# Query projection of a hybrid encoder block: the rotary channels of all heads in one channel tile

## The chip, the cores and the metric

The kernel runs on one core of a Trainium2 chip. The metric is the device time of one launch in microseconds, on the slowest core, which here is the only one. TensorE (PE) does the matmuls, VectorE (DVE), ScalarE (ACT) and GpSimd (POOL) the work on vectors, and SyncE (SP) issues nearly all DMA transfers, in one queue.

## The reference, cut to what matters

One encoder block over S = 2048 tokens of width 1024, all in float32: a combined projection feeds windowed attention (8 query heads of 64 channels, 2 key/value heads) and a bidirectional chunked scan (SSD, 16 chunks of 128 tokens); both are normed, projected out and added, and a convolved gated feed-forward part (FFN) follows. What bears on the change is the partial rotary embedding: only the first 16 of a head's 64 channels are turned.

```
def apply_partial_rope(t, cos, sin):
    half = ROT_DIM // 2                      # ROT_DIM = 16, head width 64
    t1, t2, rest = t[..., :half], t[..., half:ROT_DIM], t[..., ROT_DIM:]
    return jnp.concatenate([t1 * c - t2 * s, t2 * c + t1 * s, rest], axis=-1)
...
    h = rmsnorm(x, norm1_g[l])
    proj = h @ w_in[l]
    q, k, v, z, xbc, dt_raw = jnp.split(proj, IN_SPLITS, axis=-1)
    attn = rmsnorm(windowed_attention(q, k, v, ...), attn_out_g[l])
```

## The kernel before

**Matmuls.** Every float32 operand is split into a high part (rounded to the matmul's type) and the low rest, and each product is three matmuls: high x high, high x low, low x high (`mm3`, L105 to L108). A split is an ACT cast and a subtraction on DVE or POOL; for weights these are L141 and L142.

**Tiles and halves.** The tokens are worked in two halves of 1024. The projection runs by channel tiles of 128 columns: eight for the scan's inputs (`C0` to `C7`, `conv_unit`), tile 8 for the keys, and tiles 9 to 12 for the queries, two heads of 64 channels in each. One tile and 512 tokens are a bank, 128x512 in PSUM (`pj`, or `pq` where two tiles are made together). `tok_pair` makes values, gates and time steps for 256 tokens (`tp` banks, L500 to L502).

**Rotary work.** `rope_bank` (L417 to L466) takes a bank of tiles 8 to 12. It loads a table of cosines and sines for all 128 rows (`cs`, 512 KB, L425; rows that are not turned have cosine 1 and sine 0). In half 0 the table is multiplied by the tokens' norm factor r (L428), which half 1 has in its input already. The sine half of a work tile `rw` is set to zero on POOL (L430), the bank is copied to its other half (ACT, L431), and four DMAs of 8 rows each bring the partner channels to their place (L433, L434). DVE multiplies the bank by the cosines, which frees PSUM (L436). `flush()` then runs what earlier banks had deferred, and the bank defers its own tail: POOL multiplies by the sines and adds (L446, L447), then the sum is split. A head has 64 rows, and its high and low parts shall lie above each other in 128 rows, so each bank takes two casts and two subtractions over 64x512 (L441, L443) and one write of 512 KB to `qs_d` (L454). Attention loads its chunk of 128 tokens from there (`aq`, L700). The key bank writes to `ks_d` (L463, L464) from more pieces.

**Buffers.** `rw` comes from a ring of five work buffers (`t1024`) that many stages share. `cs` comes from that ring, or, by the bank, from the two buffers `qs` and `ks` in which attention also holds its `aq` and `ak`.

**Order.** Two strings (`PLAN`) say in which order the units of each half are written down: `R8` to `R12` are rotary tiles, `W` and `t` the token work, `b`, `s` steps of the scans, `a` steps of attention, `H` and `Q` the out-projection; `P3` makes tiles 11 and 12 for the last 512 tokens, and the same pair for the 512 before them comes in the first feed-forward units. A scheduler then fixes one order per engine from its own model of durations, so a change in one place can move instructions of other stages. Half 0 has ten rotary banks (two each for tiles 11, 10, 12, 9, 8), half 1 ten more.

**Other names.** L571 to L641 are steps of the time-step chain and the scans' states, L735 to L780 attention, L875 and L880 the decay matrices `ab` of the scan (eight DVE steps of 128x128, then one exponential on ACT), L885 to L936 the scan's outputs, L997 the out-projection's sum, L1022 and L208 the second norm's product and split.

## Time and profile before

| | us |
|---|---|
| three runs | 2496.54, 2498.95, 2504.64 (median 2498.95) |
| the profiled execution | 2505.61 |
| its span | 2503.8 |
| PE busy | 2373.5 (95%) |
| DVE, POOL, ACT busy | 1761.6, 1126.9, 1088.3 |

The span is the time between the first and the last instruction of the one execution that was recorded; the 1.8 us more are launch and end. All times below are from that execution, in us from the start of its span. The projection of half 0 takes until about 240 us, half 1 with attention, scans and out-projection until about 690; what follows is the feed-forward part, with the rest of attention and scans beside it.

### The profile page before, as it was taken

The numbers are of one execution on the slowest core, as the hardware profiler recorded it, in microseconds if no ns is written. First come the engines' busy times: TensorE is split into PE (matmuls) and PEld (weight loads), VectorE is DVE, ScalarE is ACT, GpSimd is POOL, SyncE is SP. The second block draws the span as 40 slices with busy tenths as digits, with TensorE's granted clock in tenths as the row PEclk, the third lists the DMA queues.
The fourth block names the chain that finished last, engine by engine and source line by source line (L and its number), as shares of the span: only waits on it lengthen the run. The fifth ranks groups of instructions, "written<-read, shape, count | busy, mean of one in ns | idle before, by whom it ended". The sixth has DMA issues, their size and how long they took to land.

```text
span 2503.8 us, 31565 instructions
## 1 busy us (share of the span) xinstructions
PE 2373.5 (95%) x11440; PEld 1975.7 (79%) x11440; DVE 1761.6 (70%) x3116; ACT 1088.3 (43%) x1814; POOL 1126.9 (45%) x625
## 2 busy tenths in 40 slices
PE   8998999887899999999999999999999999999997
PEld 6877798766688887777788777777888877788887
DVE  5778778878786775468978685689686555844445
ACT  5444565444354444335444443254444433433334
POOL 1045314564545435445444443554444445544444
PEclk9999999998899999999999999999999999999998
DMA  6567445774433343333434333343443232332232
GB/s 225 178 198 224 126 147 186 247 246 149 141 116 122 127 140 97 101 112 122 126 131 137 99 133 114 90 129 119 129 127 96 84 114 89 118 101 93 93 94 84
DMA packets 176047, 332.13 MB, mean 133 GB/s; under 512 B 13202, under 2 KB 84242, under 8 KB 175892
## 3 DMA queue, kind: packets, MB, share of 16 engines
q1 hardware_dynamic: 175892, 330.12, 41.2%
q8 instruction: 90, 1.47, 0.2%
q14 instruction: 65, 0.53, 0.1%
HBM read 284.06 MB, written 44.71 MB: 131 GB/s over the span
## 4 chain that ended last, share of the span: by engine, by line
PE 50%; DVE 9%; POOL 2%; issue 2%; ACT 1%; DMA 1%; DVEq 0%; POOLq 0%; SPq 0%; ACTq 0%
PE up_b L108 9%; PE up_b L107 9%; PE up_b L106 9%; PE dn_b L106 3%; PE dn_b L107 3%; PE dn_b L108 3%; DVE fa L1047 2%; POOL wlo L142 2%; PE dn L107 2%; PE dn L106 2%; PE dn L108 2%; PE wo_b L108 2%; PE wo_b L106 2%; PE wo_b L107 2%; DVE m_lo L972 1%
## 5 line engine op out<-in xcount | busy, mean ns | idle before, releaser
L142 POOL TENSOR_TENSOR wlo<-wraw,whi 128x1024 fp32r<-128x1024 f32 (+1 forms) x306 | 739.0, 2416 | 901.8 <-ACT whi L141 849.8
L108 PE MATMUL up_b<-h_hi,wlo 128*128 128x512 f32 x1392 | 555.3, 399 | 15.9 <-POOL wlo L142 15.8
L107 PE MATMUL up_b<-h_lo,whi 128*128 128x512 f32 x1392 | 553.0, 398 | 4.7 <-DVE h_lo L208 4.7
L106 PE MATMUL up_b<-h_hi,whi 128*128 128x512 f32 x1392 | 554.3, 399 | 1.4 <-ACT whi L141 0.9
L141 ACT CAST whi<-wraw 128x1024 fp32r<-128x1024 f32 (+1 forms) x330 | 338.9, 1027 | 453.0 <-PE up_b L107 117.8
L1047 DVE SCALAR_TENSOR_TENSOR fa<-up_b,fcw,fa 128x511 f32<-128x511 f32 (+2 forms) x396 | 271.4, 686 | 206.1 <-ACT fa L1049 201.7
L108 PEld LDWEIGHTS up_b<-h_hi,wlo 128*128 128x128 f32 x1392 | 264.6, 190 | 79.8 <-POOL wlo L142 21.8
L107 PEld LDWEIGHTS up_b<-h_lo,whi 128*128 128x128 f32 x1392 | 264.3, 190 | 63.3 <-DVE h_lo L208 5.9
L106 PEld LDWEIGHTS up_b<-h_hi,whi 128*128 128x128 f32 x1392 | 264.1, 190 | 60.1 <-ACT whi L141 2.3
L106 PE MATMUL dn_b<-f,whi 128*128 128x512 f32 x528 | 211.4, 400 | 0.4 <-DVE x L1090 0.2
L107 PE MATMUL dn_b<-f,whi 128*128 128x512 f32 x528 | 208.8, 395 | 0.0
L108 PE MATMUL dn_b<-f,wlo 128*128 128x512 f32 x528 | 204.3, 397 | 0.0
L1069 ACT ACTIVATE fth<-fa 128x512 f32<-128x512 f32 (+1 forms) x88 | 55.6, 632 | 217.3 <-DVE fa L1047 165.3
L1074 ACT CAST f<-fth 128x512 fp32r<-128x512 f32 (+1 forms) x88 | 54.4, 620 | 207.6 <-DVE fth L1071 169.2
L1090 DVE TENSOR_TENSOR x<-x,dn_b 128x512 f32<-128x512 f32 x144 | 97.5, 680 | 61.0 <-PE dn_b L108 60.9
L1049 ACT ACTIVATE fa<-up_b,fcw 128x512 f32<-128x512 f32 x176 | 136.0, 774 | 0.2
L106 PEld LDWEIGHTS dn_b<-f,whi 128*128 128x128 f32 x528 | 99.7, 189 | 22.8 <-DVE x L1090 1.1
L108 PEld LDWEIGHTS dn_b<-f,wlo 128*128 128x128 f32 x528 | 99.3, 188 | 22.4 <-POOL wlo L142 0.3
L107 PEld LDWEIGHTS dn_b<-f,whi 128*128 128x128 f32 x528 | 99.2, 188 | 21.2
L875 DVE SCALAR_TENSOR_TENSOR ab<-ab,ldt,mask 128x128 f32<-128x128 f32 x256 | 106.7, 482 | 11.7 <-DMA ab<-acs_d 11.5
L1075 DVE TENSOR_TENSOR f<-fth,f 128x512 fp32r<-128x512 f32 (+1 forms) x88 | 79.2, 900 | 30.3 <-ACT f L1074 29.4
L106 PE MATMUL pj_b<-h_hi,whi 128*128 128x512 f32 x208 | 85.4, 411 | 12.3 <-ACT h_hi L235 7.1
(328 smaller groups left out, 5047.1 us busy)
## 6 DMA issues: line engine op xcount, KB each, us to landing
wraw<-in_w_up SPq DMA_DIRECT2D x176, 512.0 KB
wraw<-in_w_dn SPq DMA_DIRECT2D x64, 512.0 KB
wraw<-in_w_out SPq DMA_DIRECT2D x36, 512.0 KB
ab<-acs_d SPq DMA_DIRECT2D x32, 512.0 KB
wraw<-in_w_ch SPq DMA_DIRECT2D x28, 512.0 KB
wraw<-in_w_dn SPq DMA_DIRECT2D x32, 384.0 KB
ak<-ks_d SPq DMA_DIRECT2D x14, 768.0 KB
cs<-in_rope SPq DMA_DIRECT2D x20, 512.0 KB
```

The lines of the kernel that those rows point to most:

```text
L106: nc.tensor.matmul(ps, whi, xhi, start=first, stop=False)
L107: nc.tensor.matmul(ps, whi, xlo, start=False, stop=False)
L108: nc.tensor.matmul(ps, wlo, xhi, start=False, stop=last)
L141: A.copy(hi[:, :m], raw[:, :m])
L142: (V if i < WV or i in WVS else G).tensor_tensor(lo[:, :m], raw[:, :m], hi[:, :m].bitcast(F32), ALU.subtract)
L875: (G if i < SUBP[0 if first else 1] else V).scalar_tensor_tensor(ab[:, i, d], ab[:, i, d], ldt[:, d, c, h : h + 1], mask3[:, 2 * d * P : ( ...
L1047: V.scalar_tensor_tensor(o, src, w(q), o, ALU.mult, ALU.add)
L1049: A.activation(ai[:, 0:TB], u, AF.Identity, bias=w(3), scale=w(2))
L1069: A.activation(th[:, :n], acc[:, 0, :n], AF.Tanh)
L1074: A.copy(fs[:, idx, 0, :n], th[:, :n])
L1075: V.tensor_tensor(fs[:, idx, 1, :n], th[:, :n], fs[:, idx, 0, :n].bitcast(F32), ALU.subtract)
L1090: V.tensor_tensor(xv, xv, ps[i], ALU.add)
```

## The change

The host lays out the query columns differently. Tile 9 now holds the 16 rotary channels of all eight heads: rows 0 to 63 the first eight of each head, rows 64 to 127 the second eight. Tiles 10, 11 and 12 hold channels 16 to 31, 32 to 47 and 48 to 63 of all heads, and nothing in them is turned.

A bank of tiles 10 to 12 goes to the new `plain_bank`. In half 0 DVE multiplies it by r into a work tile `hl`; ACT casts, DVE subtracts, each once over 128x512, at once and not deferred; in half 1 both read the PSUM bank itself. Two writes of 256 KB (8 heads x 16 rows x 512 tokens) put high and low part in their rows of `qs_d`, whose layout is as before but for the order of the rows within a head's high and low part. There is no table, no zeroing, no swap and no POOL step. A bank of tile 9 has a table of its own (`ropeq`), two swaps of 64 rows instead of four of 8, no zeroing, one cast and one subtraction over 128x512, and four writes of 128 KB. Key banks (tile 8) are as before. Twelve of the sixteen query banks are plain. Over the kernel 12 table loads and 56 swaps go and 24 writes come.

```diff
--- before.py
+++ after.py
@@ -414,7 +414,23 @@
 
         pend.append(tail)
 
+    def plain_bank(ci, t0, u):
+        ts = slice(t0, t0 + 512)
+        half = t0 // 1024
+        hl = t1024(f"hl{ci}_{t0}").rearrange("p (a n) -> p a n", a=2)
+        if half in rbc:
+            V.tensor_tensor(hl[:, 1], u, rbc[half][:, t0 % 1024 : t0 % 1024 + 512], ALU.mult)
+            u = hl[:, 1]
+        flush()
+        A.copy(hl[:, 0].bitcast(F32R), u)
+        V.tensor_tensor(hl[:, 1].bitcast(F32R), u, hl[:, 0], ALU.subtract)
+        for s in range(2):
+            r0 = 64 * s + 16 * (ci - 9)
+            nc.sync.dma_start(qs_d[:, r0 : r0 + 16, ts], hl[:, s])
+
     def rope_bank(ci, t0, u, cs_tag=None):
+        if ci > 9:
+            return plain_bank(ci, t0, u)
         ts = slice(t0, t0 + 512)
         half = t0 // 1024
         if cs_tag is None:
@@ -422,16 +438,17 @@
         else:
             cs = bp.tile([P, 1536 if cs_tag == "ks" else 1024], F32, tag=cs_tag, name=f"cs{ci}_{t0}")[:, :1024]
         cs = cs.rearrange("p (a n) -> p a n", a=2)
-        nc.sync.dma_start(cs, a["rope"][:, :, ts])
+        nc.sync.dma_start(cs, a["rope" if ci == 8 else "ropeq"][:, :, ts])
         if half in rbc:
             r = rbc[half][:, t0 % 1024 : t0 % 1024 + 512]
             V.tensor_tensor(cs, cs, r.unsqueeze(1).broadcast_to([P, 2, 512]), ALU.mult)
         rw = t1024(f"rw{ci}_{t0}").rearrange("p (a n) -> p a n", a=2)
-        G.memset(rw[:, 1], 0.0)
+        if ci == 8:
+            G.memset(rw[:, 1], 0.0)
         A.copy(rw[:, 0], u)
-        for b in (0, 64):
-            nc.sync.dma_start(rw[b : b + 8, 1], rw[b + 8 : b + 16, 0])
-            nc.sync.dma_start(rw[b + 8 : b + 16, 1], rw[b : b + 8, 0])
+        for b, n in ((0, 8), (64, 8)) if ci == 8 else ((0, 64),):
+            nc.sync.dma_start(rw[b : b + n, 1], rw[b + n : b + 2 * n, 0])
+            nc.sync.dma_start(rw[b + n : b + 2 * n, 1], rw[b : b + n, 0])
         q = cs[:, 0]
         V.tensor_tensor(q, u, q, ALU.mult)
         flush()
@@ -447,11 +464,12 @@
             eng(16).tensor_tensor(q, q, rw[:, 1], ALU.add)
             lo, up = slice(0, 64), slice(64, 128)
             if ci != 8:
-                for e, (r0, r1) in enumerate(((lo, up), (up, lo))):
-                    put(rw[r0, e], q[r0])
-                    put(rw[r1, e], q[r0], rw[r0, e])
-                i = 2 * (ci - 9)
-                nc.sync.dma_start(qs_d[i : i + 2, :, ts].rearrange("a p t -> p a t"), rw)
+                put(rw[:, 0], q)
+                put(rw[:, 1], q, rw[:, 0])
+                for s in range(2):
+                    for z, rows in enumerate((lo, up)):
+                        r0 = 64 * s + 8 * z
+                        nc.sync.dma_start(qs_d[:, r0 : r0 + 8, ts], rw[rows, s])
                 return
             kl = bp.tile([P, 6 * P], F32, tag="vt", name=f"kl{t0}")[:, :512]
             for kv, (r0, r1) in enumerate(((lo, up), (up, lo))):
@@ -1434,7 +1452,10 @@
     r = {}
     r["x"] = f["x"][0]
     r["xT"] = np.ascontiguousarray(f["x"][0].T)
-    r["w_ch"] = tile_w(np.concatenate([w_in[:, 1280:2304], w_in[:, 512:640], w_in[:, 0:512]], 1))
+    wq = w_in[:, 0:512].reshape(D, H, HD)
+    qcols = [wq[:, :, 0:16].reshape(D, H, 2, 8).transpose(0, 2, 1, 3).reshape(D, P)]
+    qcols += [wq[:, :, i : i + 16].reshape(D, P) for i in (16, 32, 48)]
+    r["w_ch"] = tile_w(np.concatenate([w_in[:, 1280:2304], w_in[:, 512:640]] + qcols, 1))
     wt = np.concatenate([w_in[:, 640:1280], w_in[:, 2304:2320]], 1)
     r["w_t"] = np.ascontiguousarray(
         wt.reshape(NK, P, 2, TW).transpose(2, 1, 0, 3)
@@ -1472,6 +1493,9 @@
     rc[:, 0:8], rc[:, 8:16] = cos, cos
     rs[:, 0:8], rs[:, 8:16] = -sin, sin
     r["rope"] = np.stack([rc.reshape(P, S), rs.reshape(P, S)], 1)
+    qc = np.tile(cos, (2 * H, 1))
+    qsn = np.concatenate([np.tile(-sin, (H, 1)), np.tile(sin, (H, 1))], 0)
+    r["ropeq"] = np.ascontiguousarray(np.stack([qc, qsn], 1), dtype=np.float32)
     return r
 
 
```

What the scheduler makes of it is shown at three places, before and after apart (of L numbers above 430 the new file's are 16 to 18 higher).

DVE near the end of half 0's projection, before: `cs9` and `cs8` are the tables of R9 and K (the number behind is the bank's first token), `cacc` a convolution of tile 6.

```order
L436 TENSOR_TENSOR cs9_512_1635<-pj9_0_b1_1580,cs9_512_1635 128x512
L142 TENSOR_TENSOR wlo_1672<-wraw_1585,whi_1671 128x1024
L428 TENSOR_TENSOR cs9_0_1647<-cs9_0_1647,rx_half_150 128x1024
L366 SCALAR_TENSOR_TENSOR cacc6_0_1522<-cu6_0_1519,cacc6_0_1522 128x1024
L627 MEMSET stateb_3449 128x512
L436 TENSOR_TENSOR cs9_0_1647<-pj9_0_b0_1579,cs9_0_1647 128x512
L443 TENSOR_TENSOR rw9_512_1638<-cs9_512_1635,rw9_512_1638 64x512 x2
L443 TENSOR_TENSOR rw9_0_1650<-cs9_0_1647,rw9_0_1650 64x512 x2
L142 TENSOR_TENSOR wlo_2122<-wraw_1675,whi_2121 128x1024
L428 TENSOR_TENSOR cs8_512_1725<-cs8_512_1725,rx_half_150 128x1024
L436 TENSOR_TENSOR cs8_512_1725<-pj8_0_b1_1670,cs8_512_1725 128x512
```

The same place after:

```order
L453 TENSOR_TENSOR cs9_512_1563<-pj9_0_b1_1508,cs9_512_1563 128x512
L366 SCALAR_TENSOR_TENSOR cacc6_0_1457<-cu6_0_1454,cacc6_0_1457 128x1024
L444 TENSOR_TENSOR cs9_0_1572<-cs9_0_1572,rx_half_150 128x1024
L645 MEMSET stateb_3373 128x512
L142 TENSOR_TENSOR wlo_1595<-wraw_1513,whi_1594 128x1024
L453 TENSOR_TENSOR cs9_0_1572<-pj9_0_b0_1507,cs9_0_1572 128x512
L460 TENSOR_TENSOR rw9_512_1566<-cs9_512_1563,rw9_512_1566 128x512
L444 TENSOR_TENSOR cs8_0_1667<-cs8_0_1667,rx_half_150 128x1024
L460 TENSOR_TENSOR rw9_0_1575<-cs9_0_1572,rw9_0_1575 128x512
L444 TENSOR_TENSOR cs8_512_1648<-cs8_512_1648,rx_half_150 128x1024
L453 TENSOR_TENSOR cs8_512_1648<-pj8_0_b1_1593,cs8_512_1648 128x512
```

The scaling of `cs9_512` is no longer in the neighbourhood (it is 17th on the engine), R9's four subtractions are two, and K's first table is scaled ahead of R9's last subtraction.

SP's queue at the same place, before: the swaps of K's bank, R9's writes and K's tables.

```order
L434 DMA rw8_512_1728<-rw8_512_1728 8x512
L454 DMA qs_d_103<-rw9_512_1638 128x2x512
L425 DMA cs8_512_1725<-in_rope 128x2x512
L433 DMA rw8_512_1728<-rw8_512_1728 8x512
L434 DMA rw8_512_1728<-rw8_512_1728 8x512
L454 DMA qs_d_103<-rw9_0_1650 128x2x512
L425 DMA cs8_0_1743<-in_rope 128x2x512
```

After:

```order
L441 DMA cs8_0_1667<-in_rope 128x2x512
L450 DMA rw9_0_1575<-rw9_0_1575 64x512
L451 DMA rw9_0_1575<-rw9_0_1575 64x512
L472 DMA qs_d_103<-rw9_512_1566 8x8x512 x4
L441 DMA cs8_512_1648<-in_rope 128x2x512
L450 DMA rw8_512_1651<-rw8_512_1651 8x512
L451 DMA rw8_512_1651<-rw8_512_1651 8x512
L450 DMA rw8_512_1651<-rw8_512_1651 8x512
L451 DMA rw8_512_1651<-rw8_512_1651 8x512
L472 DMA qs_d_103<-rw9_0_1575 8x8x512 x4
```

One of K's tables is now ahead of R9's second swaps; the other stands behind four writes.

DVE in half 1, where tile 10's and tile 9's banks lie beside attention chunk 3 and the first scan chunks (`ab0`, `ab1`: their decay matrices), before:

```order
L443 TENSOR_TENSOR rw10_1024_4115<-cs10_1024_4113,rw10_1024_4115 64x512
L875 SCALAR_TENSOR_TENSOR ab1_0_4256<-ab1_0_4256,ldt_85,mask3_141 128x128 x6
L443 TENSOR_TENSOR rw10_1024_4115<-cs10_1024_4113,rw10_1024_4115 64x512
L875 SCALAR_TENSOR_TENSOR ab1_0_4256<-ab1_0_4256,ldt_85,mask3_141 128x128 x2
L436 TENSOR_TENSOR cs9_1536_4198<-pj9_1_b1_4143,cs9_1536_4198 128x512
L780 TENSOR_TENSOR am3_3693<-po3_1_3966,ao3_1_4016 64x256 x2
L875 SCALAR_TENSOR_TENSOR ab1_1_4258<-ab1_1_4258,ldt_85,mask3_141 128x128 x8
L516 SCALAR_TENSOR_TENSOR zth0_1_0_4314<-zth0_1_0_4314,tp0_1_0_b0_4264 128x200
L790 TENSOR_REDUCE ass3_4234<-asq3_4232 128x128
L622 TENSOR_TENSOR statef0_4036<-statef0_4036,stf0_4130 128x512
L436 TENSOR_TENSOR cs9_1024_4215<-pj9_1_b0_4142,cs9_1024_4215 128x512
```

After:

```order
L893 SCALAR_TENSOR_TENSOR ab0_0_3930<-ab0_0_3930,ldt_85,mask3_141 128x128 x8
L645 MEMSET statef_3911 128x512
L893 SCALAR_TENSOR_TENSOR ab0_1_3932<-ab0_1_3932,ldt_85,mask3_141 128x128 x8
L708 TENSOR_TENSOR sb5_3884<-sb5_3884,pbt5_3885 128x512
L453 TENSOR_TENSOR cs9_1536_4105<-pj9_1_b1_4050,cs9_1536_4105 128x512
L798 TENSOR_TENSOR am3_3617<-po3_0_3697,ao3_0_3880 64x256 x2
L785 TENSOR_TENSOR pl3_1_1_3907<-pt3_1_1_3900,ph3_1_1_3905 128x512
L785 TENSOR_TENSOR pl3_1_2_3920<-pt3_1_2_3913,ph3_1_2_3918 128x512
L453 TENSOR_TENSOR cs9_1024_4112<-pj9_1_b0_4049,cs9_1024_4112 128x512
L798 TENSOR_TENSOR am3_3617<-po3_1_3890,ao3_1_3940 64x256 x2
L893 SCALAR_TENSOR_TENSOR ab1_0_4151<-ab1_0_4151,ldt_85,mask3_141 128x128 x8
```

Tile 10's two subtractions (now L426, 475th and 480th on the engine) have left the neighbourhood, and both of tile 9's cosine products stand ahead of `ab1`, where they stood behind and within it.

## Rows read from the trace of the kernel before

**Rows 1.** The page's part 1: busy time, share of span, instructions.

```profile
PE 2373.5 (95%) x11440; PEld 1975.7 (79%) x11440; DVE 1761.6 (70%) x3116; ACT 1088.3 (43%) x1814; POOL 1126.9 (45%) x625
```

**Rows 2.** Stretches of the span: us, each engine's busy us, mean clock, DMA share, GB/s.

```profile
160.00:240.00 80.00, 68.84 (x338) 58.11 (x336) 71.53 (x92) 34.44 (x60) 45.84 (x35) 0.96 0.69 221
223.80:230.60 6.80, 3.25 (x12) 3.25 (x13) 4.66 (x5) 1.61 (x4) 2.55 (x2) 0.50 0.90 284
450.00:690.00 240.00, 193.50 (x957) 162.78 (x957) 197.00 (x311) 103.05 (x190) 138.52 (x98) 0.89 0.59 189
690.00:1100.00 410.00, 407.23 (x1850) 332.32 (x1849) 269.00 (x463) 175.13 (x286) 188.32 (x94) 1.00 0.37 119
```

**Rows 3.** PE's waits by releaser, 160 to 240 us: total, times, longest us.

```profile
PE tp_b L500 <- DVE cs L436: 6.7, 2, 6.4
PE stb L618 <- POOL xsbb L633: 2.6, 3, 1.0
```

**Rows 4.** PE's waits by releaser, 450 to 690 us.

```profile
PE pt L763 <- DVE mxs L737: 5.9, 1, 5.9
PE wh_b L106 <- DVE x L997: 5.0, 2, 3.4
...
PE up_b L107 <- DVE h_lo L208: 4.7, 1, 4.7
PE yo L920 <- DVE yt L921: 4.5, 1, 4.5
PE cb L885 <- DVE am L780: 3.3, 1, 3.3
PE tp_b L500 <- DVE cs L436: 2.9, 1, 2.9
```

**Rows 5.** Timeline of DVE, SP's queue and PE, 219 to 228 us: start, us, step.

```profile
219.50 0.61 SPq L425 DMA_DIRECT2D cs<-in_rope  x1
...
225.35 1.22 DVE L428 TENSOR_TENSOR cs<-cs,rx_half 128x1024 f32<-128x1024 f32 x1 [3.21 <-DMA cs<-in_rope]
...
227.35 0.64 PE L500 MATMUL tp_b<-thi,h_hi 128*128 128x328 f32 x1 [6.36 <-DVE cs L436]
```

**Rows 6.** Instructions of tile rw: ns min/median/max, first and last start.

```profile
L443 DVE TENSOR_TENSOR rw<-cs,rw x40: 674/687/1693, 141.7 to 673.1; 64x512 fp32r<-64x512 f32 x40
```

**Rows 7.** The same view of qs_d, and who waited for it (us, times).

```profile
L454 SPq DMA_DIRECT2D qs_d<-rw x16: 360/371/578, 143.2 to 674.8; - x16
...
  ACT zth L515: 4.7, 2
  ACT rw L431: 2.2, 1
  DVE dt L557: 1.7, 1
```

**Rows 8.** DVE's groups by form, 450 to 690 us: busy us, mean ns, idle before.

```profile
L443 DVE TENSOR_TENSOR rw<-cs,rw 64x512 fp32r<-64x512 f32 x20 | 20.4, 1022 | 2.4 <-ACT rw L441 1.9
...
L436 DVE TENSOR_TENSOR cs<-pj_b,cs 128x512 f32<-128x512 f32 x6 | 4.1, 684 | 2.3 <-ACT rw L431 2.3
```

**Rows 9.** POOL's groups by form, 450 to 690 us.

```profile
L447 POOL TENSOR_TENSOR cs<-cs,rw 128x512 f32<-128x512 f32 x10 | 14.7, 1467 | 0.3 <-DVE cs L436 0.2
```

**Rows 10.** Timeline of DVE at four places between 462 and 665 us.

```profile
462.43 2.39 DVE L443 TENSOR_TENSOR rw<-cs,rw 64x512 fp32r<-64x512 f32 x2
...
473.56 8.10 DVE L875 SCALAR_TENSOR_TENSOR ab<-ab,ldt,mask 128x128 f32<-128x128 f32 x6
481.69 1.64 DVE L443 TENSOR_TENSOR rw<-cs,rw 64x512 fp32r<-64x512 f32 x1
...
551.73 6.27 DVE L875 SCALAR_TENSOR_TENSOR ab<-ab,ldt,mask 128x128 f32<-128x128 f32 x8
...
660.94 3.14 DVE L443 TENSOR_TENSOR rw<-cs,rw 64x512 fp32r<-64x512 f32 x2
```

**Rows 11.** ACT's longest wait by releaser, 0 to 700 us.

```profile
ACT ab L880 <- DVE ab L875: 45.0, 11, 10.3
```

## The prediction

> **What bounds the kernel now.** I read the page first. TensorE (PE) is busy 95% of the span, VectorE (DVE) 70%, GpSimd (POOL) and ScalarE (ACT) under half [rows 1]. The change takes nothing from PE: the weight columns are only put in another order. So it can pay only where PE stands still or is granted its lower clock, near rotary work. The table of stretches says where that is [rows 2]. From 690 to 1100 us PE is busy 407 of 410 us at full clock; nothing is to be had there, and after the first feed-forward units the order of instructions is the same in both kernels. Two places are left. **Place A**, 160 to 240 us, is the end of half 0's projection: PE is busy 68.8 of 80 us. **Place B**, 450 to 690 us, holds half 1's rotary banks beside attention, the scans and the out-projection: PE is busy 193.5 of 240 us, the mean granted clock is 0.89, DVE is busy 197 us. There 46.5 us of PE are idle; and a mean of 0.89 between full speed (2.4 GHz) and half (1.2 GHz) means some 0.11/0.5 x 240 = 53 us at the lower level. Third, PE's waits by releaser: A has 6.7 us on the cosine product L436, all but 0.3 of it once, and 2.6 us on a scan step [rows 3]; B's idle time is spread over a dozen releasers, mostly DVE (the six that the sum needs stand in [rows 4]), of which one alone, with 2.9 us, is rotary by name.
>
> **Place A, step by step.** The 6.4 us wait is a chain of K's bank [rows 5]: its table is issued at 219.50, since its buffer is freed by R9's tail; it lands when DVE starts scaling it at 225.35 (5.85 us); the scaling takes 1.22, the product 0.7, and only then are PSUM banks free for the token matmuls at 227.35. Around it the clock is at 0.50 for 6.8 us, with 3.25 us of work in them [rows 2], so about 3.25/2 = 1.6 us more are lost.
> What the change takes from this chain: R10 to R12 load no tables, do no scaling and no POOL work, so R9 is not queued behind them; R9's own tail has one full-height subtraction per bank instead of two half-height ones (median 0.69 us each [rows 6]). In the new order K's first table is issued ahead of R9's second swaps, and the scaling of R9's first bank has left this place on DVE. What it adds: the second table stands behind four writes instead of one. An issue of such a write takes 0.36 to 0.58 us [rows 7], so 1.1 to 1.7 us more; I take 1.4. The new multiplication by r (one 128x512 DVE operation per plain bank, read from PSUM) takes the place of L436, at the same price (L436 also reads a PSUM bank and one SBUF tile over 128x512: 0.68 us [rows 8]), so it is neither gain nor loss.
> I take the whole wait, 6.7, plus 1.6 of clock, less 1.4: **-7 us**. The 2.6 us on the scan step I leave at nothing, since its releaser is not rotary work; with them, and without the 1.4, it would be -11. The other end is -2: if something else holds the banks as long as the wait lasts, only the shortened splits remain.
>
> **Place B, step by step.** Six plain banks lie in half 1. Each loses L436 (0.68) and one of two half-height subtractions of 1.02 on average; two halves become one full-height operation, taken as one of 1.02, so 2 x 1.02 + 0.68 - 1.02 = 1.7 us per bank. R9's two banks lose 1.02 each. DVE: 6 x 1.7 + 2 = 12.2 us of 197 [rows 8]. POOL loses two operations of about 1.45 in each plain bank, 12 x 1.45 = 17 us (L447 1.47 [rows 9], L446 the like), and ACT one copy and one cast less per bank, of which nothing is counted, because PE's waits on ACT here are on scan and attention work.
> A rule on the price of that subtraction: the 64x512 subtraction reads two SBUF tiles and runs from 674 to 1693 ns [rows 6], long where a POOL operation runs beside it. The Trainium skill (SBUF — State Buffer, section Who interferes with whom) says that a DVE instruction with two inputs in SBUF shares a read port with a GpSimd instruction that reads SBUF, and the later one is blocked, while one with a single SBUF input is not. The new subtraction of half 1 reads PSUM and one SBUF tile; by the rule it would take 0.68 always, and DVE would lose 2 us more.
> What is on PE's path I add up from the waits in which a rotary step stands just ahead on the releaser's engine:
> - the 2.9 us on L436 [rows 4]: it stands behind a subtraction of 1.64, itself behind six L875 steps stretched to 8.10 us [rows 10]. In the new order R9's products stand ahead of chunk 1's L875 block: all 2.9.
> - the 3.3 on L780: two subtractions, 2.39 us [rows 10], stand ahead of it: 2.4.
> - the 4.5 on L921: two subtractions, together 3.14 us, stand shortly ahead of it [rows 10]: 3.1.
> - the 4.7 on L208: its DVE steps lie beside R11's and R12's last POOL operations, and a POOL neighbour can more than double a DVE step [rows 6]: about half, 2.
> - the 5.0 on L997: its longer part is other work; 1.6 of it, the wait at 558 us, comes behind eight L875 that took 6.27 us [rows 10] while POOL ran L446 and L447: 1.6.
> - the 5.9 on L737 (attention scores): chunk 4's scores move forward in the order, as no table holds the attention buffers: half, 3.
> That is 15 us of gaps. Of the clock: the lower level lies around the gaps, so I count half of the 46.5 idle us into its 53 (an estimate); the other 30 us are work that costs 15 us more than at full clock, and with a third of the gaps gone I give back a third of that: 5. Together 20. These gaps have next-latest releasers (the L875 blocks, the scans' copies), of which I know only that twelve kinds end the waits now; I take a third off: **-13 us**. The ends: 0, if each gap is filled by its next releaser, and -30, if all 15 us of gaps and the whole 15 us of clock come back.
>
> **Sum.** -7 - 13 = -20 us against the profiled execution's 2505.6, so 2485.6. The median of the runs, 2498.95, lies 6.7 below that execution; on that scale the forecast is **2479 us** (-0.8%). What the change does outside A and B I cost at nothing: in 0 to 160 and 240 to 450 PE's waits are on conversions, norms and scans, and 6 MB of tables that are not loaded run beside matmuls that don't wait for them. If that cover goes it is a small gain, not a loss.
>
> **Rivals.**
> *No change, 2499 us.* DVE and POOL are freed, but PE's gaps in B are set by the chains of attention and the scans, which wait on ACT and DVE in turn. For it: all but one of the releasers are no rotary step by name [rows 4]. Against it: A's wait is one named chain, and B has subtractions directly ahead of three releasers.
> *Slower, 2510 us.* The split of a plain bank is no longer deferred: DVE's subtraction waits for ACT's cast of the same bank, and ACT runs in order, with exponentials that wait for DVE's L875: 45.0 us in 11 waits, the longest 10.3 [rows 11]. Where a cast stands behind such an exponential, DVE stands still at L426, L875 work behind it too, and the PSUM bank stays taken. Three banks at 10.3 are 31 us, which eats the 20 and leaves +11. It decides from three such banks on, or six at the mean of 4.1 (25 us: +5). Against it: in the new order both of R10's casts stand ahead of the first chunk's exponentials, and the other four have ten or more ACT instructions between them and the exponential before; the L875 chain would have to be late at just those places.
> *Writes land late, 2488 us.* A bank's 512 KB now leave in two writes of 8 heads x 16 rows instead of one over 128 partitions, and the work buffer is free only when they have landed. Waits on that now: 4.7 + 2.2 + 1.7 = 8.6 us on ACT and DVE [rows 7], none of them PE's. If they double and all of it reaches PE, the gain falls from 20 to 11. The Trainium skill (DMA: Bandwidth & Descriptors, section Why a DMA increments its semaphore by 16 and not by 1) says that a transfer is spread over the largest number of engines up to 16 that divides the outermost dimension on both sides; by it these writes would use 8 engines instead of 16. No row here shows the engines of one transfer.
> *More, 2458 us.* Both places give their full ends, -11 and -30: -41.
>
> **How the numbers follow.** Forecast 0.55, no change 0.18, slower 0.15, late writes 0.06, more 0.06. A measurement of this kernel tells about 0.3%, 7.5 us, from no change. Faster by more than that: the forecast, "more", and two thirds of "late writes": 0.65. Slower: "slower" but for the mild end of it: 0.12. Within: the rest, 0.23. The forecast's own range is -10 to -36, 2489 to 2463. The range that should hold 8 in 10 reaches past "no change" (2499 and its scatter) up to 2505 and down to 2460; outside are most of "slower" and "more".
>
> **What would show it.** Right, if in the new trace the token matmuls of A wait under 1 us for K's product and the clock stays up there; if B's PE busy time is the same at a stretch 10 us or more shorter, DVE some 12 us less busy; and if the waits on L208, L921 and L780 shrink. Wrong, if B's idle time is the same under other names, or if DVE's subtraction L426 shows long waits on ACT's cast L425 and PE's matmuls wait for L426.

## The result and the profile after

| | us |
|---|---|
| before, four runs beside it | median 2497.77 (2496.54 to 2504.64) |
| changed, four runs | median 2472.30 (2469.98 to 2474.65) |
| ratio | 0.9891, 95% interval 0.9876 to 0.9905 |
| forecast | 2479, range 2460 to 2505, faster 0.65 |

The change takes 25.5 us off (1.1% by the ratio). A second measurement of the same kernel on another occasion gave 2473.66 and the ratio 0.9905 (0.9887 to 0.9923). The profiled execution of the changed kernel lasted 2469.98 us, its span is 2468.1. The two profiled spans are 35.7 us apart, more than the medians, since the execution of before that was recorded lay above its median.

The page's busy times and the line of the granted clock:

```profile
PE 2356.8 (95%) x11440; PEld 1960.2 (79%) x11440; DVE 1699.9 (69%) x3088; ACT 1069.6 (43%) x1786; POOL 1082.4 (44%) x585
...
PEclk9999999998999999999999999999999999999998
```

PE's busy time falls by 17 us against [rows 1] although it does the same matmuls: in the trace of before, a 128x512 matmul is recorded with 628 ns (median) where the granted clock is 0.5 and with 393 ns where it is 1.0, and less time is spent at 0.5. DVE loses 62 us, POOL 45. The stretches of [rows 2], with the same columns (us, busy us of PE, PEld, DVE, ACT and POOL, mean clock, DMA share, GB/s):

```profile
160.00:240.00 80.00, 76.78 (x400) 67.89 (x399) 55.24 (x76) 28.52 (x57) 34.56 (x26) 0.98 0.69 212
450.00:690.00 240.00, 205.95 (x1046) 173.50 (x1045) 180.77 (x325) 106.71 (x197) 132.26 (x89) 0.93 0.55 179
690.00:1100.00 410.00, 404.94 (x1836) 329.30 (x1835) 271.04 (x450) 169.20 (x274) 192.98 (x96) 1.00 0.37 117
```

In 160 to 240 us PE is busy 76.8 instead of 68.8 us, and DVE 55 instead of 72. In 450 to 690 it is busy 206 instead of 193.5 at a clock of 0.93 instead of 0.89, but since all comes sooner, this window now holds some feed-forward work too. PE's waits, to set beside [rows 3, 4] (total, times, longest us), from 160 to 240 us:

```profile
PE stb L636 <- POOL xsbb L651: 3.2, 1, 3.2
```

and from 450 to 690 us:

```profile
PE aps L811 <- DVE ass L808: 7.8, 1, 7.8
...
PE pt L781 <- DVE mxs L755: 3.2, 1, 3.2
PE wh_b L106 <- DVE x L1015: 2.7, 1, 2.7
...
PE up_b L107 <- DVE h_lo L208: 1.9, 2, 1.3
PE yo L938 <- ACT mixed L956: 1.7, 1, 1.7
...
PE cb L903 <- DVE am L798: 1.0, 1, 1.0
```

The wait for K's product is gone, and so is the one on L436 in half 1. The waits on L780 (3.3, now L798: 1.0), L208 (4.7 to 1.9), L921 (4.5, no longer listed), L997 (5.0 to 2.7, now L1015) and L737 (5.9 to 3.2, now L755) have shrunk. One is new: 7.8 us on an attention norm's sum (L808), at a matmul where before PE waited 2.0 for another releaser. Two others have grown where they stand: 2.0 us on L785 (0.5 before, on L767), and 6.5 us once on the scan's output (L951), at a matmul that waited 4.5 before.

Windows of time hold different work in the two kernels. The number of matmuls is the same in both, so I cut by work: the time at which PE starts its 600th, 1000th, 1800th, 2800th and 3000th matmul, counted in the trace. The stretches between are: the end of half 0 (place A), the middle, the first part of place B, and its last part, with tiles 11 and 12 and the second norm. All kernels of this study stand here, in us:

```
                                   600-1000  1000-1800  1800-2800  2800-3000
before (first profile)                 94.9      153.2      234.8       53.7
before (second, b_again)               95.6      150.4      235.0       53.7
changed                                85.4      152.6      228.8       40.1
changed (second, a_again)              85.0      152.5      230.8       40.1
e1_half0  (plain in half 0 only)       85.4      152.5      236.2       54.8
e2_half1  (plain in half 1 only)      103.5      156.7      239.5       40.0
e8_nopool   (e1 less POOL's steps)     86.7      152.9      229.3       44.8
e11_nopool0 (e2 less POOL's steps)     99.4      153.4      227.8       40.0
e7_ktable (before, one buffer moved)   94.8      151.5      235.5       52.7
e3_halves                              84.3      153.4      230.0       41.1
e4_pool                                82.6      151.5      235.0       43.1
e5_table                               85.2      152.7      231.7       41.2
e6_onewrite                            84.4      151.8      225.6       41.7
e9_twowrites                           80.3      150.4      225.4       41.1
```

The change gains 10 us in the first column, about 5 in the third and 13.6 in the last; these repeat within 1 to 2 us in the second profiles. The columns are not equally good evidence. The last one is 40.0 to 43.1 us in every kernel with plain banks in half 1 and 52.7 to 54.8 with rotary ones, and 44.8 in `e8_nopool`, whose rotary banks lack POOL's steps. The third one lies anywhere between 225.4 and 239.5 us in kernels with plain banks in half 1; `e2_half1` and `e11_nopool0`, whose edits differ only in half 0, are 11.7 us apart in it. The scheduler makes a new order for every kernel, so a few us in the third column tell nothing of a cause. After the 3200th matmul the kernels run alike but for single spells of lower clock, which differ from run to run.

### The profile page after: what moved, and what is told of

Its sections match the earlier page's. It is cut to its first block, busy times and chain, and to the rows that moved or that the text cites. A ratio compares the mean times of both kernels' runs of the same rounds, so it can differ in the third digit from the quotient of the medians.

```text
span 2468.1 us, 31349 instructions
## 1 busy us (share of the span) xinstructions
PE 2356.8 (95%) x11440; PEld 1960.2 (79%) x11440; DVE 1699.9 (69%) x3088; ACT 1069.6 (43%) x1786; POOL 1082.4 (44%) x585
## 4 chain that ended last, share of the span: by engine, by line
PE 48%; DVE 10%; POOL 2%; issue 2%; ACT 2%; DMA 1%; DVEq 0%; POOLq 0%; ACTq 0%; SPq 0%
PE up_b L108 8%; PE up_b L107 8%; PE up_b L106 8%; PE dn_b L108 3%; PE dn_b L107 3%; PE dn_b L106 3%; DVE fa L1065 2%; PE dn L107 2%; PE dn L106 2%; PE dn L108 2%; PE wo_b L108 2%; PE wo_b L106 2%; PE wo_b L107 2%; POOL wlo L142 2%; DVE m_lo L990 1%
## 5 line engine op out<-in xcount | busy, mean ns | idle before, releaser
L142 POOL TENSOR_TENSOR wlo<-wraw,whi 128x1024 fp32r<-128x1024 f32 (+1 forms) x306 | 739.6, 2418 | 906.4 <-ACT whi L141 879.2
L141 ACT CAST whi<-wraw 128x1024 fp32r<-128x1024 f32 (+1 forms) x330 | 339.4, 1029 | 440.7 <-PE up_b L107 111.2
L893 DVE SCALAR_TENSOR_TENSOR ab<-ab,ldt,mask 128x128 f32<-128x128 f32 x256 | 99.7, 457 | 25.9 <-DMA ab<-acs_d 16.7
```

The costliest lines, as they stand in the source:

```text
L141: A.copy(hi[:, :m], raw[:, :m])
L142: (V if i < WV or i in WVS else G).tensor_tensor(lo[:, :m], raw[:, :m], hi[:, :m].bitcast(F32), ALU.subtract)
L893: (G if i < SUBP[0 if first else 1] else V).scalar_tensor_tensor(ab[:, i, d], ab[:, i, d], ldt[:, d, c, h : h + 1], mask3[:, 2 * d * P : ( ...
```

## The experiments

**Two controls.** The changed kernel and the kernel before, each once more.

> The changed kernel itself once more, for a second profile and for the scatter. In the pair of profiles at hand 35.7 us lie between the two spans, while the medians of the timed runs lie 25.5 apart. Scatter theory: the excess of 10 us is of the one execution of before that was recorded; this run's profile repeats the one of after, with PE's wait for K's product (tokens of half 0) absent and PE idle 38 +- 4 us between the 2000th and the 3200th matmul; time 2468 to 2476. Rival: the profile of after was a lucky one, and the second one shows 5 to 10 us more idle or low-clock time in the stretch of half 1.

> The kernel before once more, for a second profile. Scatter theory: the span comes out nearer to 2495, with less low-clock time in half 1 or at 1640 to 1700 us than the first profile (54.6 us between the 2000th and 3200th matmul), while the 6.4 us wait of the token matmuls for K's product stands as it was, being a chain of named steps. Rival: the same 2504 again.

Measured: 2473.66 us for the changed kernel; 2499.05 us and a span of 2497.3 for the one before. Both repeat their stretches (PE idle 39.6 us between the 2000th and the 3200th matmul of the changed kernel), so its first profile was no lucky one there. The two profiles of before reach the 3200th matmul at the same time and then drift 6.5 us apart, in spells of lower clock during the feed-forward part. The gain is 24 to 26 us, not 36.

**One half at a time.** The new layout throughout, but tiles 10 to 12 get rotary work back in one half, with a table of cosine 1 and sine 0. For `e1_half0`, and for `e2_half1` with 1 in place of 0:

```diff
-        if ci > 9:
+        if ci > 9 and t0 // 1024 == 0:
             return plain_bank(ci, t0, u)
...
-        nc.sync.dma_start(cs, a["rope" if ci == 8 else "ropeq"][:, :, ts])
+        nc.sync.dma_start(cs, a[{8: "rope", 9: "ropeq"}.get(ci, "ropei")][:, :, ts])
...
+            if ci > 9:
+                for e in (lo, up):
+                    put(rw[e, 0], q[e])
+                    put(rw[e, 1], q[e], rw[e, 0])
+                for s in range(2):
+                    r0 = 64 * s + 16 * (ci - 9)
+                    nc.sync.dma_start(qs_d[:, r0 : r0 + 16, ts], rw[:, s])
+                return
```

> The new layout, but tiles 10 to 12 are plain in half 0 only; in half 1 they get the rotary work back, with a table of cosine 1 and sine 0 (load, zeroing, four swaps, product, two POOL steps, two casts and two subtractions of 64x512). Theory (two places, each with its own cause): place A (160 to 240 us) gains as in the changed kernel, 9 to 12 us by the 1000th matmul, with no wait for K's product; place B (450 to 690 us) stays as before; time 10 to 13 us under before, some 2486. Rival (order: any rewriting of the schedule moves the gaps): the gain is not tied to the half; PE's idle time in half 1 differs from before by 5 us or more either way.

> The opposite: tiles 10 to 12 are plain in half 1 only, with the rotary work back in half 0 (six tables that are loaded and scaled, POOL steps, half-height splits). Theory: the wait of the token matmuls for K's product, 5 to 7 us at about 220 us, is back and place A gains under 3 us; place B gains 10 to 18 us, above all between the 2800th and 3000th matmul (13.6 us in the pair of profiles); time 12 to 18 us under before, some 2483. Rival (order): gains do not add, the sum of the two kernels' gains differs from the whole change's 25.5 us by 8 or more.

Measured: `e1_half0` 2491.53 us, ratio 0.9977 (0.9964 to 0.9989); `e2_half1` 2502.89 us, 1.0031 (1.0014 to 1.0048). In the first and the last column the theory holds: 85.4 us in the first with plain banks in half 0, and 40.0 in the last with plain banks in half 1; where a half has its rotary work back, that gain is gone. In the third column it fails, for `e2_half1` has 239.5 us there, more than before, with plain banks. By the total it fails too: 5.7 us of gain and 5.7 of loss make nothing, not 24. `e2_half1` pays 103.5 us in place A, 8 more than before, with the same wait for K's product:

```profile
PE tp_b L526 <- DVE cs L453: 8.2, 3, 6.8
PE dtp L606 <- DVE dt L597: 3.4, 1, 3.4
```

Its rotary banks of half 0 are not those of before: they leave in two writes each, and the order around them is another. Which of the two costs the 8 us was not taken apart, so I use these kernels for where a gain sits, and the pairs below for why.

**Half 1 without POOL's steps.** `e8_nopool` is `e1_half0` less the zeroing and POOL's two products in the banks of tiles 10 to 12:

```diff
-        if ci != 9:
+        if ci == 8:
             G.memset(rw[:, 1], 0.0)
...
+            if ci <= 9:
+                eng(6).tensor_tensor(rw[:, 1], rw[:, 1], cs[:, 1], ALU.mult)
+                eng(16).tensor_tensor(q, q, rw[:, 1], ALU.add)
-            eng(6).tensor_tensor(rw[:, 1], rw[:, 1], cs[:, 1], ALU.mult)
-            eng(16).tensor_tensor(q, q, rw[:, 1], ALU.add)
```

> The kernel with rotary work put back in half 1 (the earlier e1_half0), less POOL's part of it: tables, copies, swaps, cosine products and deferred splits in halves stay, the zeroing and the two POOL products per plain bank go (their table is sine 0, so nothing is lost). e1_half0 lacked the late gain of the changed kernel (13.6 us between the 2800th and 3000th matmul), with gaps of 4.7 us before the second norm's low part and of 5.1 us before the scan's output. Theory (POOL's steps beside the norm are the cause of both): both gaps are gone, time 9 to 14 us under e1_half0, near the changed kernel. Rival (the deferred DVE subtractions are the cause): the 5.1 us gap before the scan's output stays, with its 6.8 us of low clock; if only one gap goes, each has its own cause, and the time is 4 to 8 us under e1_half0.

Measured: 2476.79 us, ratio 0.9914 (0.9895 to 0.9934): 14.7 us under `e1_half0` and 3 to 4.5 over the changed kernel, although the tables, swaps, cosine products and half-height splits of half 1 are all still there. PE's waits from 600 to 690 us in `e1_half0`:

```profile
PE yo L946 <- DVE yt L947: 5.1, 1, 5.1
PE up_b L107 <- DVE h_lo L208: 4.7, 1, 4.7
```

and the same place in `e8_nopool`:

```profile
PE up_b L107 <- DVE h_lo L208: 2.3, 2, 1.3
```

The gap on the scan's output is gone with POOL's steps, though its releaser stood behind DVE's subtractions, and the one of 4.7 us has become two of at most 1.3. Of the 17.1 us between the two profiled spans, 10.0 lie in the last column (54.8 to 44.8), in which kernels with the same kind of banks differ by 3 at most; 6.9 lie in the third, where that tells nothing. The timeline of `e1_half0` shows what happens in the last stretch (start, us, step), first DVE:

```profile
637.47 6.18 DVE L1048 SCALAR_TENSOR_TENSOR h2t<-x,gv,r 128x512 f32<-128x512 f32 x3
...
646.72 2.63 DVE L1048 SCALAR_TENSOR_TENSOR h2t<-x,gv,r 128x512 f32<-128x512 f32 x1
...
650.97 2.89 DVE L1048 SCALAR_TENSOR_TENSOR h2t<-x,gv,r 128x512 f32<-128x512 f32 x1
653.78 3.25 DVE L460 TENSOR_TENSOR rw<-cs,rw 64x512 fp32r<-64x512 f32 x2
657.07 0.75 DVE L1048 SCALAR_TENSOR_TENSOR h2t<-x,gv,r 128x512 f32<-128x512 f32 x1
```

and POOL beside it:

```profile
637.39 1.27 POOL L463 TENSOR_TENSOR rw<-rw,cs 128x512 f32<-128x512 f32 x1 [3.44 <-DMA rw<-rw]
638.62 2.81 POOL L142 TENSOR_TENSOR wlo<-wraw,whi 128x1024 fp32r<-128x1024 f32 x1
641.39 1.71 POOL L464 TENSOR_TENSOR cs<-cs,rw 128x512 f32<-128x512 f32 x1
...
644.74 1.72 POOL L463 TENSOR_TENSOR rw<-rw,cs 128x512 f32<-128x512 f32 x1
646.43 2.37 POOL L142 TENSOR_TENSOR wup<-wraw,wup 128x1024 fp32r<-128x1024 f32 x1
648.76 1.73 POOL L464 TENSOR_TENSOR cs<-cs,rw 128x512 f32<-128x512 f32 x1
```

The same place on DVE in `e8_nopool`, where POOL is still until 634.61:

```profile
631.47 2.07 DVE L1049 SCALAR_TENSOR_TENSOR h2t<-x,gv,r 128x512 f32<-128x512 f32 x3
```

The norm's first three products take 6.18 us beside L463, L142 and L464 on POOL, and 2.07 with POOL still. Rotary steps are not the only such neighbours: the two long ones, 2.63 and 2.89 us, ran for most of their time beside weight splits L142, which stand behind L463 and L464 in POOL's order, and in `e8_nopool` two products beside L142 took 5.06. The subtractions at 653.78, which need L464's sum, land in front of the scan's steps; in `e8_nopool` they stand earlier and spread out. How much of the 10 us is the stretching and how much this other order was not taken apart. The norm's product by form, from 450 to 700 us (count, busy us, mean ns), in the kernel before:

```profile
L1022 DVE SCALAR_TENSOR_TENSOR h2t<-x,gv,r 128x512 f32<-128x512 f32 x8 | 13.3, 1695 | 0.0
```

In `e1_half0`:

```profile
L1048 DVE SCALAR_TENSOR_TENSOR h2t<-x,gv,r 128x512 f32<-128x512 f32 x8 | 13.9, 1761 | 0.0
```

In `e8_nopool`:

```profile
L1049 DVE SCALAR_TENSOR_TENSOR h2t<-x,gv,r 128x512 f32<-128x512 f32 x8 | 10.4, 1331 | 0.0
```

In the changed kernel:

```profile
L1040 DVE SCALAR_TENSOR_TENSOR h2t<-x,gv,r 128x512 f32<-128x512 f32 x8 | 9.8, 1249 | 0.0
```

So 3.5 us of DVE's time in steps that are no rotary work go with POOL's steps. The scan's decay steps (L875 before) don't follow them: 45.9 us in `e1_half0`, 39.0 in `e8_nopool`, but 43.4 in the changed kernel and 54.3 in `e3_halves`, which is as fast.

**POOL's steps alone on the changed kernel.** `e4_pool` gives each plain bank a deferred tail with two POOL products, and writes after it:

```diff
+        def tail():
+            for _ in range(2):
+                G.tensor_tensor(hl[:, 1], hl[:, 1], hl[:, 1], ALU.mult)
```

> The changed kernel with POOL's two steps per plain bank kept (two 128x512 products in a deferred tail, low part times itself, after which the bank's writes go out; the low part of the plain rows is lost by that). DVE, ACT, tables and swaps as changed. Theory (the gap of 4.7 us before the second norm's low part, and the lower clock behind it, came from DVE steps stretched beside POOL's last rotary steps): that gap is back with 3 to 5 us, the low-clock time of the late stretch with 7 us, and the time is 5 to 9 us over the changed kernel; place A stays without its wait. Rival (POOL's steps were hidden, DVE's own removed work is all): within 3 us of the changed kernel, the late gap stays near 1.3 us.

Measured: 2479.35 us, ratio 0.9931 (0.9915 to 0.9946), 5 to 7 us over the changed kernel, as expected in size and not in place: the last stretch rises only by 3 us (40.1 to 43.1), the one before it by 4 to 6, and the gap before the norm's low part stays small. These steps are lighter than rotary ones (a tile times itself takes 1.04 us in the median, 1.40 for L447 before), need no swap, and come sooner after their bank. So these products, with the order that comes with them, cost 5 to 7 us; only the last stretch tells them from the order, by 1.4 to 3 us (it is 40.0 to 41.7 in the other kernels with plain banks). That the whole 10 us of the last stretch need POOL's steps in the rotary bank's chain is not shown.

**The splits by halves.** `e3_halves` splits plain banks in two times 64 rows.

```diff
-        A.copy(hl[:, 0].bitcast(F32R), u)
-        V.tensor_tensor(hl[:, 1].bitcast(F32R), u, hl[:, 0], ALU.subtract)
+        for e in (slice(0, 64), slice(64, 128)):
+            A.copy(hl[e, 0].bitcast(F32R), u[e])
+            V.tensor_tensor(hl[e, 1].bitcast(F32R), u[e], hl[e, 0], ALU.subtract)
```

> The changed kernel, but each plain bank is split in two halves of 64 rows (two casts and two subtractions of 64x512 instead of one each of 128x512); everything else as changed. Theory (the late gain of half 1, 13.6 us between the 2800th and 3000th matmul, comes from POOL's steps and from subtractions that stood deferred ahead of the scan's and the norm's steps): the late gain stays, since the doubled subtractions (12 more of 0.69 us on DVE) stand where the banks are made and not in tails; time 0 to 4 us over the changed kernel. Rival (DVE's subtraction time itself is the price): each doubled subtraction counts, 6 x 0.7 in half 1 and as much in half 0, and the time goes up 6 to 9 us with PE's waits on L426's neighbours growing.

Measured: 2474.30 us, ratio 0.9910 (0.9896 to 0.9925): no difference from the changed kernel. Twelve more subtractions of 0.7 us on DVE cost nothing that can be measured.

**The table loads.** `e5_table` loads each plain bank's old table into its old buffer, and nothing reads it.

```diff
+            tab = t1024(f"tab{ci}_{t0}") if cs_tag is None else bp.tile(...)
+            nc.sync.dma_start(tab.rearrange("p (a n) -> p a n", a=2), a["rope"][:, :, t0 : t0 + 512])
             return plain_bank(ci, t0, u)
```

> The changed kernel, but each plain bank also loads its 512 KB table into the buffer that it had before (nothing reads it). So the twelve table loads and the buffers' holding are back, without scaling, products, POOL or swaps. Theory (place A's wait is K's table issued late, because buffers and tails of the banks before it free its buffer late): a small part returns, under 3 us at the token matmuls of half 0, since no tail holds the tables; in half 1 attention chunk 4 is late again by the buffers; time 0 to 5 us over the changed kernel. Rival (traffic: 6 MB less to load is what made place A faster): 8 us or more of place A's 11.5 come back.

Measured: 2474.69 us, ratio 0.9907 (0.9891 to 0.9923): the same as the changed kernel. The 6 MB don't carry the gain of place A (85.2 us in the first column), nor do the buffers, as far as they are held only until the load has landed.

**K's table.** `e7_ktable` is the kernel before with one buffer moved, so that K's first table needn't wait for tile 9's tail.

```diff
-            rope_bank(ci, half * 1024 + b * 512, ps[b], ("qs" if half else None, "ks")[b])
+            rope_bank(ci, half * 1024 + b * 512, ps[b], ("qs" if half else None, None if (ci, half) == (9, 0) else "ks")[b])
```

> The kernel before with one edit: in half 0 the first table of tile 9 comes from the ring of work buffers instead of the buffer ks, so that K's first table finds ks free as soon as tile 12's bank has left it, and is issued ahead of tile 9's work. Nothing else is removed. Theory (place A's wait is the chain: buffer freed by the tail of tile 9, load of 5.9 us, scaling, product): the 6.2 to 6.4 us wait of the token matmuls for K's product falls to under 2 us, or moves to K's other bank at less, the 1000th matmul comes 5 to 9 us sooner, and the time is 4 to 9 us under before. Rival (the chain only ends last: DVE's and POOL's rotary work ahead of it is as late): the wait stays at 5 us or more and the time is within 3 us of before.

Measured: 2496.67 us, ratio 0.9995 (0.9986 to 1.0004): nothing. The rival holds by its numbers, for the wait only changed its name:

```profile
PE tp_b L500 <- DVE thi L528: 5.3, 1, 5.3
...
PE tp_b L500 <- DVE cs L436: 1.2, 1, 1.2
```

The 6.4 us on K's product are 1.2 now, and 5.3 us stand on the values' step L528, 24 matmuls later. That step is short; what it waited for shows in DVE's order:

```profile
223.52 3.21 DVE L443 TENSOR_TENSOR rw<-cs,rw 64x512 fp32r<-64x512 f32 x2 [3.21 <-ACT rw L441]
227.08 1.23 DVE L428 TENSOR_TENSOR cs<-cs,rx_half 128x1024 f32<-128x1024 f32 x1 [0.35 <-DMA cs<-in_rope]
228.23 0.34 DVE L528 SCALAR_TENSOR_TENSOR thi<-tp_b,xcols,thi 128x128 fp32r<-128x128 f32 x1
```

Two subtractions of tile 9's tail and the scaling of a table stand ahead of it. That table is the one of K's second bank, which is issued late now in place of the first:

```profile
221.77 0.61 SPq L425 DMA_DIRECT2D cs<-in_rope  x1
```

So the edit freed one of K's two banks and left the other late. Times of both, counted from the 600th matmul's start, in us (issue of the table, start of the cosine product):

```
              K's first bank    K's second bank   1000th
              table   product   table   product   matmul
before         79.5    86.6      82.4    90.7      94.9
e7_ktable      67.3    80.4      83.9    91.2      94.7
e2_half1       88.3    94.4      92.3   100.8     103.5
e11_nopool0    80.9    86.9      87.5    95.6      99.4
changed        64.2    76.1      68.9    78.4      85.4
```

In the four slow ones the 1000th matmul comes 2.7 to 4.2 us behind the product of K's second bank. In the changed kernel that product comes 12 us sooner than before, the matmul 9.5.

**Half 0 without POOL's steps.** `e11_nopool0` is `e2_half1` with the edit of `e8_nopool`.

> The mirror of e8_nopool: the kernel with rotary work put back in half 0 (the earlier e2_half1, 2502.9 us, wait of 6.8 us for K's product), less POOL's part of it (zeroing and two products per plain bank; their table is sine 0, so nothing is lost). Tables, their scaling on DVE, copies, swaps, cosine products and deferred splits in halves stay in half 0. Theory now (in half 1 POOL's steps were the cause; place A, where DVE was busy 71.5 of 80 us before and 55.2 after, is bound by DVE's own rotary work): the wait for K's product stays at 4 us or more, place A gains at most 4 us of its 11.5, time 2485 to 2497. Rival (POOL again: its steps hold the tails of tiles 12 and 9 and so DVE's splits and the buffers behind them): the wait falls under 2 us, place A gains 8 us or more, time 2473 to 2482.

Measured: 2485.25 us, ratio 0.9956 (0.9939 to 0.9973): 17.6 us under `e2_half1`, and in the range that the theory gave, but not by its mechanism. The wait for K's product is gone (0.2 us), as the rival had it, and the first column is still 99.4 us, 4 more than before:

```profile
PE stb L645 <- POOL xsbb L660: 4.7, 2, 4.2
PE tp_b L527 <- DVE thi L555: 4.0, 1, 4.0
PE stb L645 <- issue: 2.1, 1, 2.1
```

The time is lost on the token pair's values again and on the scans' states, whose loads stand in SP's queue among tables and swaps (POOL waits 8.7 us for them, but 6.7 in the changed kernel too). DVE is busy only 56.3 of 80 us here, as in the changed kernel, so it isn't the sum of DVE's time that binds place A. Its order does again: the values' step L555 stands right behind the scaling of K's second table.

```profile
234.31 1.23 DVE L444 TENSOR_TENSOR cs<-cs,rx_half 128x1024 f32<-128x1024 f32 x1
235.45 0.35 DVE L555 SCALAR_TENSOR_TENSOR thi<-tp_b,xcols,thi 128x128 fp32r<-128x128 f32 x1
```

So K's tables are late without POOL's steps too. Nor do the 17.6 us lie in place A: 4 do, 3 in the second column, and 11.7 in the third, where both kernels have plain banks.

**The writes.** `e6_onewrite` orders `qs_d` by channel row, then head, and the query columns within a tile likewise, so that a bank leaves in one write of 128 rows x 2 x 512. `e9_twowrites` has the same layout and two writes of 128x512.

```diff
-    qs_d = dram("qs_d", [H, P, S])
+    qs_d = dram("qs_d", [P, H, S])
...
-            nc.sync.dma_start(qs_d[:, r0 : r0 + 16, ts], hl[:, s])
+        nc.sync.dma_start(
+            qs_d.rearrange("(s r) h t -> r h s t", s=2)[r0 : r0 + 16, :, :, ts].rearrange("r h s t -> (r h) s t"), hl
+        )
...
-    qcols = [wq[:, :, 0:16].reshape(D, H, 2, 8).transpose(0, 2, 1, 3).reshape(D, P)]
-    qcols += [wq[:, :, i : i + 16].reshape(D, P) for i in (16, 32, 48)]
+    qcols = [wq[:, :, i : i + 16].transpose(0, 2, 1).reshape(D, P) for i in (0, 16, 32, 48)]
```

> The changed kernel with the query buffer in DRAM laid out by channel row, then head, and the query columns within a tile ordered the same way, so that a bank's high and low part leave in one write of 128 rows x 2 x 512 again (16 writes instead of 40). Theory (the 24 more writes lie in SP's queue beside other work and land in time): within 3 us of the changed kernel. Rival (the writes in pieces land late and hold work buffers, or delay what stands behind them in SP's queue): 4 to 10 us faster than the changed kernel, with shorter waits for the write of the query buffer on ACT and DVE.

> The layout of e6_onewrite, which was 9 us faster than the changed kernel, but high and low part of each bank leave in two writes of 128x512 (32 writes instead of 16; the changed kernel has 40, of 8 x 16 x 512 or 8 x 8 x 512, whose issue takes 0.58 us on SP against 0.37 for the one write). Theory (what counts is the landing of writes in pieces of 8 heads, and their dear issue): as e6_onewrite within 3 us. Rival (the number of transfers in SP's queue counts): half or more of e6_onewrite's 9 us is lost. A third, that e6_onewrite's gain was a chance of the new order: the time lies anywhere between 2464 and 2477 and the trace shows no shorter wait for the query buffer.

Measured: `e6_onewrite` 2464.68 us, ratio 0.9871 (0.9854 to 0.9888); `e9_twowrites` 2461.77, 0.9855 (0.9838 to 0.9871). Both beat the changed kernel, by 8 to 9 and by 10 to 12 us, and `e9_twowrites` is the fastest kernel of this study, 36 us under before. The number of writes is not it, since 32 do no worse than 16. Their form shows on SP's queue, in the view of the tile `qs_d` (ns min/median/max of an issue). In the changed kernel:

```profile
L429 SPq DMA_DIRECT2D qs_d<-hl x24: 567/584/1075, 130.8 to 626.3; - x24
```

In `e6_onewrite`:

```profile
L419 SPq DMA_DIRECT2D qs_d<-hl x12: 359/377/419, 131.9 to 622.5; - x12
```

In `e9_twowrites`:

```profile
L420 SPq DMA_DIRECT2D qs_d<-hl x24: 319/326/1948, 133.9 to 619.6; - x24
```

With the writes of tile 9 that is 40 x 0.58 = 23 us of SP's time against 16 x 0.37 = 6 and 24 x 0.33 + 8 x 0.39 = 11; against that, attention's 16 loads from the new layout take 0.53 to 0.54 us each to issue instead of 0.38. But the engines that waited for such a write (ACT 1.7 us in the changed kernel, 1.3 and 1.8 in the others) waited no less, and the gain sits in no one place: 3 to 5 us in the third column, where the order alone does as much, and up to 5 in the first. Whether it is SP's time, the landing or the new order stays open.

## Why the prediction came out right, step by step

**What bounds the kernel: right.** Both places that the stretches of [rows 2] named are where the time went, and nothing came after the first feed-forward units. About half of the gain lies in the last 54 us of place B alone.

**Place A, -7: the size was too small, the chain right but told for half of it.** It measured -10. I had put the wait down to one chain, the table of K's first bank behind tile 9's tail [rows 3, 5]. `e7_ktable` moved that table, and 5.3 of the 6.4 us came back behind the second one. The change brings both sooner, and so the whole wait went, as I took it. That was in part luck: I had counted the second table only as a cost of 1.4 us behind four writes, and what waits if it stays late only as the -2 end. By size: PE's idle time between the 600th and the 1000th matmul falls from 11.2 and 10.0 us (two profiles) to 3.2 and 3.0. That is 7.5, the 6.7 on K's product and 1.6 on a time step (L571) that I had not counted, less 1 on the scan step. The other 2.5 are clock, where I had 1.6; of the 1.4 for the writes nothing shows. Which of the things taken away (tables, scaling, swaps, copies, splits) makes K's tables early is not shown. Of those tried alone, halved splits, two POOL products or the table loads put back don't cost the gain (`e3_halves`, `e4_pool`, `e5_table`), and POOL's steps taken out don't bring it (`e11_nopool0`). The scan step that I left at nothing (2.6 us) is 3.2 now, at another spot, so that choice was right.

**Place B, -13: it measured -18.7**, about -5 before the 2800th matmul and -13.6 behind it. Term by term against [rows 4]: L436, forecast 2.9, gave 2.9; L780, 2.4, gave 2.3; L921, 3.1, gave all of its 4.5; L208, 2, gave 2.8; L997, 1.6, gave 2.3; L737, 3, gave 2.7. That is 17.5 of gaps against 15. But other waits grew, the 5.8 us more on L808 first among them: PE's whole idle time between the 1800th and the 3000th matmul falls only from 49.7 and 51.9 us (two profiles) to 38.1 and 39.7, by 12. The forecast had 10 left of its 15 after the third that it took off for the next releasers, so that step held. Mis-sized was the clock: 3 were left of the 5 forecast, and 7 came. The time at clock 0.5 falls from 54.6 and 47.8 us to 37.5, in the last stretch alone from 13.7 to 0. The releasers in B are of sixteen kinds, not twelve, which changes nothing in the sum.

**Where the terms came from: wrong in two.** I counted POOL's 17 us [rows 9] as lying off the path, but for two gaps, and gave L921's gap to the length of DVE's subtractions [rows 10]. `e8_nopool` keeps all the half-height subtractions of the tails and has no such gap; it shows that POOL's steps are worth 10 us in the last stretch: DVE's steps beside them are stretched, and the subtractions that need their sums come late, in front of others' work. `e3_halves` agrees as far as it goes: twelve subtractions more, though not in tails, cost nothing. What the 5 us of the third column come from is open.

**The subtraction's price: right.** The new L426 reads PSUM and one SBUF tile in half 1, and two SBUF tiles in half 0 (first row); ns min/median/max:

```profile
L426 DVE TENSOR_TENSOR hl<-hl x6: 680/684/1346, 130.8 to 171.9; 128x512 fp32r<-128x512 f32 x6
L426 DVE TENSOR_TENSOR hl<-pq_b,hl x4: 676/681/691, 514.4 to 625.6; 128x512 fp32r<-128x512 f32 x4
L426 DVE TENSOR_TENSOR hl<-pj_b,hl x2: 681/686/692, 438.5 to 442.3; 128x512 fp32r<-128x512 f32 x2
```

It never exceeds 0.69 us in half 1, though three of the six ran beside a POOL operation from start to end; in half 0 the one that overlaps POOL reaches 1.35, the other five don't overlap it and take 0.68 to 0.69. The 1.02 that I took for it was 0.34 too dear, 2 us in all. The Trainium skill (SBUF — State Buffer, section Who interferes with whom), by which one SBUF input doesn't meet GpSimd's reads and two do, is borne out here, and by the norm's product above, which reads two SBUF tiles and takes 0.75 us alone and up to 2.9 beside POOL. Had I applied it to the steps that stay on DVE, and not only to the new one, it would have pointed at the last stretch as a place where POOL's 17 us are paid.

**The rivals.** "No change" fell: releasers without rotary names were late because of rotary work ahead of them on their engine or beside it on POOL, shown for K's second bank and for the last stretch, argued for the rest. "Slower" came only in part: in half 1 L426 waited 4.3 us for ACT's cast, 4.0 of it once, and PE waited 0.8 us for L426. That one cast stood behind a weight cast L141 that waited for PE, not behind an exponential; three waits of 10.3 did not come. "Writes land late" was wrong as it was told, since the waits on the query buffer fell (ACT's from 4.7 [rows 7] to 1.7 us), but `e6_onewrite` and `e9_twowrites`, with another form of the writes, are 8 to 12 us faster; whether the form is why, or the new order, is not shown. An issue takes 0.58 us, the upper end of the range that I took from [rows 7]. That such a write uses 8 of 16 engines, the rule of the Trainium skill (DMA: Bandwidth & Descriptors, section Why a DMA increments its semaphore by 16 and not by 1) beside that rival, is shown by no run here.

**The sum.** -20 was forecast, 24 to 25.5 measured: place A and B each gave more, and the range held. The profiles show more than the timed medians: their 3200th matmul comes 30 us sooner on average, 28.7 of it in A and B and 3.6 ahead of the 600th, less 2.4 in the stretches between and behind. The recorded executions of before lay above its median, those of the changed kernel near or below theirs. The 3.6 us stand in a stretch that differs by 5 us among the kernels here and are put down to nothing.

## What to carry over

A wait with one clear name may be only the last of several that are equally late: move that one cause alone and see whether the wait goes or changes its name, before it is counted as a gain. Where the name changes, look at what stands ahead of the new releaser on its engine: a step of 0.34 us ended a wait of 5.3 here, behind the same kind of work one bank later. And where every kernel gets a new order, find a stretch that stays put under unrelated edits before a few us are read as an effect. An operation on an engine that has time to spare is not free where its neighbour shares something with it; look at the spread between the shortest and the longest duration of one form, and at what ran beside the long ones. When a layout is chosen for the arithmetic, try the order of the buffer in DRAM with it: the kernels whose writes cover all 128 partitions were 8 to 12 us faster here.

## What the runs showed of the hardware

- DVE's product over 128x512 with two SBUF inputs took 0.74 to 0.75 us with POOL still and 1.7 to 2.9 beside POOL's steps (`e1_half0`, 630 to 670 us); a subtraction with one input in PSUM stayed at 0.68 to 0.69 us in six of six cases, three of them beside POOL (changed kernel). It is not always the product that is stretched: one in the changed kernel (at 644.43) took 0.73 us beside a split on POOL, and that split took 3.52 us, where others took 1.3.
- Issuing a write of 8 x 16 x 512 elements took 0.58 us of SP's queue, one of 128 x 2 x 512 0.37 and one of 128 x 512 0.33, whatever the bytes: 256, 512 and 256 KB.
- The kernel before ran between 2491.4 and 2507.4 us over all comparisons; its two profiles differ by 6.5 us, none of it in the gaps that the change removes.
